# Two row-block pairs of the way up computed plainly, rows in memory laid out by operand, and the last group of the way down added on the chip

## The chip, the cores and the metric

The kernel runs on one core of a Trainium2 chip. The metric is the device time of one execution in microseconds. Before the change it was 2530.95 us as a median of three runs (2529.95 to 2533.86). The engines are named as in the profile: PE (TensorE, matmuls; PEld its weight loads), DVE (VectorE), ACT (ScalarE), POOL (GpSimd), SP (SyncE, which here issues DMAs).

## The reference

One step of a hybrid encoder layer for 1024 tokens of a prompt and 64 tokens of a running stream. The part that the change touches is the end of the layer, a gated feed-forward network with a short causal convolution:

```python
mix = jax.nn.sigmoid(gate_ssm) * (y_ssm @ p['w_branch_ssm']) + jax.nn.sigmoid(gate_att) * (o @ p['w_branch_attn'])
x = x + mix @ p['w_out']

h = _rmsnorm(x, p['norm_ffn_w']) @ p['w_up']
ha, hb = jnp.split(h, 2, axis=-1)
hc, ffn_new = _causal_dwconv(ffn_past, ha, p['ffn_conv_w'], p['ffn_conv_b'])
x = x + (jax.nn.silu(hc) * hb) @ p['w_down']
```

`D_MODEL` is 1024, `D_FF` is 2816, the convolution is three wide, and everything is float32.

## The kernel before

*Layout.* Tokens are columns, features are rows: the 1088 tokens lie side by side, and a tile holds 128 features. In the FFN the columns are cut into four quarters of 272 (`QW`); a half is two quarters. Quarter `2 * v + s` is quarter `s` of half `v`.

*Precision.* A float32 operand is split in two: `hi` is a cast by ACT to the matmul's rounded type, `lo` is the difference of the operand and `hi`, by DVE (`split`, L840 to L842). Each product of two tiles is three matmuls: hi·hi, hi·lo and lo·hi.

*Seven products for eight.* The FFN's two matrix products are done in blocks of two by two with seven products instead of eight (the Strassen-Winograd scheme). On the way up, an item is a pair: row block `f` of `w_up` and row block `f + 22`, the convolution's side and the gate's. The inner dimension has two halves of four tiles, the columns two halves. The right-hand operands (`PARTS`) are `b11`, `t2`, `b21`, `t3`, `t1`, `t4` and `b22`: quarters of x1, or sums and differences of them, made by `differences` (L895 to L905), split by `part`, and kept on the chip in the homes of a table (`home`; units are named n0 to n11 and m000 to m311). The left-hand operands are weight blocks or sums of them: `left_parts` loads two blocks of 512 KB, makes four sums on POOL (L918, L919, L929, L936) and splits seven operands of 128 x 512. A pair is 7 products x 2 quarters x 4 tiles x 3 = 168 matmuls of 272 columns.

*From x1 to the FFN.* `output(m, qs)` computes row block `m` of x1 for the quarters `qs`, adds the input, stores the rows to `yT` and has POOL add up squares. `norm(q)` multiplies the sum by a block of ones on PE (L875), and ACT and DVE make the reciprocal root (L211 to L215, with loads of activation tables, since Ln, Exp and Square alternate); then DVE scales eight tiles (L882). `first_half` does this for quarters 0 and 1 and splits `b11` and `b21` between the outputs of quarters 2 and 3. Quarters 2 and 3 are normed behind the last output. Pairs 0 and 1 are begun with their products p0 (`b11`) and p2 (`b21`), which need quarters 0 and 1 alone; their other five products need differences.

*A pair's end.* `pair(f)` takes each product's sum from PSUM with ACT or DVE (L1059 to L1078), `gate` applies the convolution and silu (an affine step on ACT, two on DVE, silu on ACT), `put` multiplies with the gate's side on POOL (L1051) and stores a half row block to `h_sc`.

*The way down.* The 22 hidden row blocks form three groups, `DOWN` = 8, 8 and 6. Each group is four items of two output row blocks, again seven products. `hidden_sums` loads the stored rows, makes the four right-hand sums on POOL (L989 to L992) and stores them to `t_sc`. `hidden_part(g, name)` loads the rows of an operand of the next group (`hr`), casts them on ACT (L1010) and subtracts on DVE, for the second quarter beyond the first two tiles on POOL (L1011). That is done while the last item of the previous stage runs, part by part, into the homes that its products leave. `pair_down` adds its results onto `yT` in memory by accumulating DMAs, issued by POOL (L1092), 48 in all, 16 per group.

*What sets the order.* The code names the engine of each instruction. A scheduler orders the instructions of each engine by the program's order, by priorities and by its own model of durations; each engine then runs its row in order. All loads and plain stores are issued by SP.

Of the kernel before, what the change touches and what calls it, by code (L numbers as in the profile page):

```python
# [9 lines left out]
F32 = mybir.dt.float32  # L10
# [7 lines left out]
P = 128  # L18
# [57 lines left out]
def hybrid_layer(ctx: ExitStack, tc: tile.TileContext, xT, prm, cst, rope, wvd, win, wbs, wba, wout, wup, wdn,  # L76
# [19 lines left out]
    h_sc = scratch("h_sc", [DFF, T])  # L96
    t_sc = scratch("t_sc", [4 * DFF // 2, T // 2])
# [792 lines left out]
    def differences(s, eng):  # L890

        b11, b21, b12, b22 = x1[s][:2], x1[s][2:], x1[2 + s][:2], x1[2 + s][2:]
        t2 = [couple(row("fs", "t2")) for _ in range(2)]
        for j in range(2):
            eng.tensor_tensor(out=b11[j], in0=b12[j], in1=b11[j], op=ALU.subtract)  # L895
        for j in range(2):
            V.tensor_tensor(out=t2[j], in0=b22[j], in1=b11[j], op=ALU.subtract)
        part("t2", s, t2)
        for j in range(2):
            G.tensor_tensor(out=b12[j], in0=b22[j], in1=b12[j], op=ALU.subtract)  # L900
        part("t1", s, b11)
# [4 lines left out]
        part("b22", s, b22)  # L906
# [67 lines left out]

# [3 lines left out]
    h3 = h_sc.rearrange("(f p) t -> p f t", p=P)  # L978
    t3 = t_sc.rearrange("(k f p) t -> p k f t", k=4, p=P)
    KIND = ("t1", "t2", "t3", "t4")  # L980

    def hidden_sums(i):

        b11, b12, b21, b22 = (row("fb", n)[:, :HALF] for n in ("g11", "g12", "g21", "g22"))
        e = row("fb", "ge")[:, :HALF]
        for u, (x, y) in enumerate(((b11, b12), (b21, b22))):
            for v, t in enumerate((x, y)):
                load(out=t, in_=h3[:, 2 * i + u, HALF * v : HALF * (v + 1)])
# [4 lines left out]
        for n, t in zip(KIND, (e, b11, b12, b21)):  # L993
            load(out=t3[:, KIND.index(n), i], in_=t)
# [138 lines left out]
    for at in early:  # L1133
        pairs[0].send(at)
        if at[1] == 1 and at[0] == 0:
            more_left(1)
# [133 lines left out]
```

## Time and profile before

| | |
|---|---|
| median of 3 runs | 2530.95 us (2529.95 to 2533.86) |
| the profiled execution | 2527.61 us |
| its span | 2525.8 us |
| mean granted TensorE clock | 0.986 |
| PE busy | 2440.0 us (97%), 16910 matmuls |
| DVE busy | 1612.5 us (64%) |
| ACT busy | 1184.8 us (47%) |
| POOL busy | 723.2 us (29%) |
| bytes moved | 399.15 MB |

Busy times are sums over one execution. The output stage ends at about 1760 us, the way up at about 2270 us, the way down with the span. A row of the timeline gives start, duration, engine, line, operation, output and inputs, the count of like instructions, and in brackets how long the engine stood before it and what ended that. A row by stretch gives the stretch, its length, and busy time and count of each engine, the granted clock, the share of the DMA engines and GB/s.

### The profile page before, as it was taken

What the parts mean: (1) busy time and instruction counts of PE and PEld (TensorE: products, weight loads), DVE (VectorE), ACT (ScalarE), POOL (GpSimd) and SP (SyncE); (2) the same over time, 40 slices, a digit from 0 to 9 for tenths busy, and PEclk for the clock granted to TensorE, in tenths of its full rate; (3) what the DMA queues carried; (4) which work ended last, traced back from release to release, by engine and by line L of the source; (5) the groups of instructions that cost most, each with busy time, mean ns of one, the idle gap of its engine ahead of it and who ended that gap; (6) DMA issues with size and microseconds to landing.
All of it is one profiled execution on the core that took longest, in us unless ns stands there. A gap on an engine that the chain in (4) does not pass through costs nothing. (4 is left out here: it accounts for less than half of the span.)

```text
span 2525.8 us, 44652 instructions
## 1 busy us (share of the span) xinstructions
PE 2440.0 (97%) x16910; PEld 2358.9 (93%) x16910; DVE 1612.5 (64%) x2724; ACT 1184.8 (47%) x2574; POOL 723.2 (29%) x745
## 2 busy tenths in 40 slices
PE   8999999999999999999999998998699999998998
PEld 8999999999999999998889898998699999998998
DVE  6326255854777667447667764645877777786764
ACT  6234243644666455357655754225443434343542
POOL 3000000100111001014433240024476676666543
PEclk9999999999999999999999999999799999999999
DMA  5217158545354354255697745663134333467875
GB/s 165 79 57 275 68 217 246 163 137 152 110 150 138 110 147 117 88 193 175 204 342 240 235 128 198 203 195 107 39 123 140 122 140 120 141 206 185 205 162 97
DMA packets 261911, 399.15 MB, mean 158 GB/s; under 512 B 32288, under 2 KB 190112, under 8 KB 261568
## 3 DMA queue, kind: packets, MB, share of 16 engines
q1 hardware_dynamic: 254784, 382.93, 47.3%
q0 software_dynamic: 6912, 13.37, 3.7%
q8 instruction: 133, 2.18, 0.4%
q14 instruction: 82, 0.67, 0.1%
HBM read 262.65 MB, written 133.56 MB: 157 GB/s over the span
## 5 line engine op out<-in xcount | busy, mean ns | idle before, releaser
L149 PE MATMUL mm<-xn_hi,w_hi 128*128 128x384 f32 (+1 forms) x1416 | 470.3, 332 | 0.9 <-DVE zr L431 0.9
L151 PE MATMUL mm<-xn_hi,w_lo 128*128 128x384 f32 (+1 forms) x1416 | 468.3, 331 | 0.5 <-DVE w_lo L143 0.5
L150 PE MATMUL mm<-xn_lo,w_hi 128*128 128x384 f32 (+1 forms) x1416 | 467.1, 330 | 0.0
L149 PEld LDWEIGHTS mm<-xn_hi,w_hi 128*128 128x128 f32 x1416 | 266.6, 188 | 5.3 <-issue 2.0
L151 PEld LDWEIGHTS mm<-xn_hi,w_lo 128*128 128x128 f32 x1416 | 266.7, 188 | 3.0 <-issue 0.8
L150 PEld LDWEIGHTS mm<-xn_lo,w_hi 128*128 128x128 f32 x1416 | 266.6, 188 | 1.8 <-issue 0.6
L143 DVE TENSOR_TENSOR w_lo<-w_f,w_hi 128x1024 fp32r<-128x1024 f32 (+1 forms) x120 | 152.7, 1273 | 127.6 <-ACT w_hi L142 127.1
L1023 PE MATMUL mx<-n,wh 128*128 128x272 f32 x1156 | 222.0, 290 | 6.2 <-ACT u L1101 2.3
L1023 PE MATMUL mx<-m,w_hi 128*128 128x272 f32 x1114 | 214.4, 290 | 7.0 <-DVE down L1109 5.3
L1023 PEld LDWEIGHTS mx<-n,wh 128*128 128x128 f32 x1156 | 182.8, 190 | 7.3 <-ACT u L1101 2.8
L142 ACT CAST w_hi<-w_f 128x1024 fp32r<-128x1024 f32 (+1 forms) x120 | 125.7, 1049 | 131.2 <-PE mm L150 74.5
L1023 PEld LDWEIGHTS mx<-m,w_hi 128*128 128x128 f32 x1114 | 177.3, 191 | 7.6 <-issue 5.1
L1023 PE MATMUL mx<-n,wl 128*128 128x272 f32 x578 | 167.2, 290 | 0.0
L1023 PE MATMUL mx<-m,w_lo 128*128 128x272 f32 x557 | 161.6, 290 | 0.0
L149 PE MATMUL mm<-b_hi,w_hi 128*128 128x384 f32 (+1 forms) x448 | 147.3, 330 | 6.5 <-DVE b_g L193 3.4
L151 PE MATMUL mm<-b_hi,w_lo 128*128 128x384 f32 (+1 forms) x448 | 146.5, 327 | 0.0
L150 PE MATMUL mm<-b_lo,w_hi 128*128 128x384 f32 (+1 forms) x448 | 146.3, 327 | 0.0
L448 POOL COPY pre<-pre 128x3 f32<-128x3 f32 x48 | 13.1, 273 | 456.3 <-ACT pre L449 332.5
L549 ACT ACTIVATE p_t<-sc,mx 128x1024 f32<-128x1024 f32 (+5 forms) x144 | 106.0, 738 | 76.6 <-DVE mx L540 36.5
L460 DVE SCALAR_TENSOR_TENSOR cc<-pre,par,cc 128x384 f32<-128x384 f32 (+1 forms) x216 | 126.5, 586 | 23.5 <-ACT cc L458 18.4
L841 ACT CAST w_hi<-ws 128x512 fp32r<-128x512 f32 (+1 forms) x68 | 41.4, 608 | 169.6 <-PE mx L1023 122.9
L842 DVE TENSOR_TENSOR wl<-w_f,wh 128x512 fp32r<-128x512 f32 (+1 forms) x102 | 94.7, 928 | 30.3 <-ACT wh L841 29.6
(346 smaller groups left out, 6730.2 us busy)
## 6 DMA issues: line engine op xcount, KB each, us to landing
w_f<-in_win_dram SPq DMA_DIRECT2D x76, 512.0 KB, 3.7
w_f<-in_wup_dram SPq DMA_DIRECT2D x44, 512.0 KB, 3.7
bc<-a_sc SPq DMA_DIRECT2D x32, 512.0 KB, 6.3
out_dram<-down POOLq DMA_DIRECT2D x48, 272.0 KB, 4.9
h_sc<-hb SPq DMA_DIRECT2D x44, 272.0 KB, 2.1
g<-h_sc SPq DMA_DIRECT2D x44, 272.0 KB, 3.7
hr<-t_sc SPq DMA_DIRECT2D x40, 272.0 KB, 4.7
x_sc<-cc SPq DMA_DIRECT2D x48, 192.0 KB, 2.1
```

The costliest lines, as they stand in the source:

```text
L142: S.copy(hi, w)
L143: V.tensor_tensor(out=lo, in0=w, in1=hi, op=ALU.subtract)
L149: PE.matmul(ps, a_hi, b_hi, start=i == 0, stop=False)
L150: PE.matmul(ps, a_hi, b_lo, start=False, stop=False)
L151: PE.matmul(ps, a_lo, b_hi, start=False, stop=i == n - 1)
L448: G.tensor_copy(pre[:, 0:3], tail)
L460: V.scalar_tensor_tensor(cc[:, :m], pre[:, i : i + m], cw(i), cc[:, :m], ALU.mult, ALU.add)
L549: act(p_t[:n, :nk], sc[c][:n, :nk], AF.Exp, bias=mx[:n, c : c + 1], accum_out=dst)
L841: S.copy(hi, src)
L842: V.tensor_tensor(out=lo, in0=src, in1=hi, op=ALU.subtract)
L1023: PE.matmul(ps, w[x][:, c], b[y][:, k], start=start and k == t == 0, stop=k == nk - 1 and t == 2, skip_group_check=not start)
```

## The change

Three things change.

1. *Pairs 0 and 1 are computed plainly*, with eight products: `pair_plain` does 192 matmuls per pair. `plain_left` loads their four weight blocks and splits them whole (128 x 1024), into the homes that `t2`, `t3` and `t4` of quarter 0 and `t2` of quarter 1 take later. The first half of each pair takes `b11` and `b21`. The second half takes `t1`, which is b12 − b11, added onto the first half's partial results, and `b22`. `first_differences` makes `t1` and splits `t1` and `b22`; `last_differences` makes and splits `t2`, `t3` and `t4`. The first halves of both pairs come first, then the last differences, then pair 2's weights, then the second halves.
2. *Rows in memory by operand.* `h_sc` and `t_sc` become one `q_sc` with eight kinds (`b11` to `b22`, `t1` to `t4`), each laid out by quarter, partition, row block and column. A load of an operand's two row blocks reads one run of 2176 B per partition, where it read two of 1088; a store of a half row and a load for `hidden_sums` now move two runs of 1088 B where they moved one of 2176. `hidden_part` subtracts on DVE throughout (21 of its 84 subtractions were on POOL).
3. *The last group of the way down is added on the chip.* Its items load their 16 half rows of `yT` early (`xr`). Product p2's two sums are taken by DVE with the addition, where ACT copied them; p3 is followed by an addition on POOL of 272 columns for each quarter, p4 and p5 by one of 544. SP stores the results; the 16 accumulating DMAs go.

On PE, the place behind the last output. Rows of `st` are the norms, n_18312, n_18585 before and n_18323, n_18596 after (with their neighbours) are `b11`, and `wh` and n_18090 to n_18097 weights of pair 0. Before:

```order
9521 L151 MATMUL mx<-m_16461,w_lo 128x272
9522 L875 MATMUL st_18733<-s_18095,con 128x272
9523 L875 MATMUL st_18790<-s_18126,con 128x272
9524 L1023 MATMUL mm<-n_18312,wh 128x272
9525 L1023 MATMUL mm<-n_18313,wh 128x272
9526 L1023 MATMUL mm<-n_18585,wh 128x272
```
After:

```order
9528 L150 MATMUL mx<-m_16460,w_lo 128x272
9529 L874 MATMUL st_18720<-s_18106,con 128x272
9530 L1095 MATMUL mm<-n_18324,n_18090 128x272
9531 L1095 MATMUL mm<-n_18323,n_18091 128x272
9532 L1095 MATMUL mm<-n_18323,n_18090 128x272
```
```order
9567 L1095 MATMUL mx<-n_18596,n_18097 128x272
9568 L1095 MATMUL mx<-n_18596,n_18096 128x272
9569 L874 MATMUL st_18751<-s_18137,con 128x272
9570 L1095 MATMUL mx<-n_18597,n_18096 128x272
9571 L1095 MATMUL mx<-n_18596,n_18097 128x272
```
The two norms stood together; now norm 3's matmul stands behind 39 plain ones.

On ACT, the same place; `sq` are squares of x1, `n` the norms' rows, `w_hi` a weight's cast. Before:

```order
1409 L841 CAST w_hi<-w_f 128x512
1410 L870 ACTIVATE sq<-x_18634 128x272
1411 L211 ACT_TABLE_LOAD
1412 L211 ACTIVATE n_18735<-st_18733,eps_t 128x272
1413 L870 ACTIVATE sq<-x_18634 128x272
1414 L212 ACT_TABLE_LOAD
1415 L212 ACTIVATE n_18736<-n_18735 128x272
1416 L213 ACTIVATE n_18735<-n_18736 128x272
1417 L211 ACT_TABLE_LOAD
1418 L211 ACTIVATE n_18792<-st_18790,eps_t 128x272
```
After:

```order
1413 L840 CAST w_hi<-w_f 128x512
1414 L869 ACTIVATE sq<-x_18645 128x272
1415 L210 ACT_TABLE_LOAD
1416 L210 ACTIVATE n_18722<-st_18720,eps_t 128x272
1417 L869 ACTIVATE sq<-x_18645 128x272
1418 L211 ACT_TABLE_LOAD
1419 L211 ACTIVATE n_18723<-n_18722 128x272
1420 L212 ACTIVATE n_18722<-n_18723 128x272
1421 L210 ACT_TABLE_LOAD
1422 L210 ACTIVATE n_18753<-st_18751,eps_t 128x272
1423 L840 CAST m_18745<-x_18409 128x544
1424 L211 ACT_TABLE_LOAD
```
The cast ahead of norm 2 is of pair 2's weights now (pair 0's before), and a cast of `b22` has come between norm 3's steps.

On POOL, after, where pair 1 ends and pair 2's weight sums begin; L1064 is `put`, L935, L936, L946 and L953 are the four weight sums:

```order
300 L1073 COPY con<-pre 128x2
301 L1048 MEMSET pre 128x2
302 L1064 TENSOR_TENSOR hb<-hb,cc 128x480
303 L1064 TENSOR_TENSOR hb<-hb,cc 128x64
304 L935 TENSOR_TENSOR ws_19086<-w_f 128x512
305 L936 TENSOR_TENSOR ws_19087<-ws_19086,w_f 128x512
306 L946 TENSOR_TENSOR w_f<-w_f 128x512
307 L953 TENSOR_TENSOR ws_19087<-w_f,ws_19087 128x512
308 L935 TENSOR_TENSOR ws_19388<-w_f 128x512
```
Before, the first weight sums behind the differences of quarters 2 and 3; L900 is a difference, L918, L919, L929 and L936 are the four sums, the first row of L936 the last sum of pair 0, the others of pair 1:

```order
294 L900 TENSOR_TENSOR x_18127<-x_18430,x_18127 128x544
295 L900 TENSOR_TENSOR x_18280<-x_18634,x_18280 128x544
296 L936 TENSOR_TENSOR ws_18702<-w_f,ws_18702 128x512
297 L1065 COPY pre<-pre 128x2
298 L918 TENSOR_TENSOR ws_18895<-w_f 128x512
299 L919 TENSOR_TENSOR ws_18896<-ws_18895,w_f 128x512
300 L929 TENSOR_TENSOR w_f<-w_f 128x512
```
Before, three of pair 0's sums stand ahead of the differences and pair 1's sums follow them; now no sum is made for pairs 0 and 1, and the first one stands behind pair 1's second `put`.

The diff, cut to its core:

```diff
@@ -887,23 +886,41 @@
             js = slice(2 * j, 2 * j + 2)
             split(hi[:, js], lo[:, js], src[j])
 
-    def differences(s, eng):
-
-        b11, b21, b12, b22 = x1[s][:2], x1[s][2:], x1[2 + s][:2], x1[2 + s][2:]
+    def quads(s):
+        return x1[s][:2], x1[s][2:], x1[2 + s][:2], x1[2 + s][2:]
+
+    def first_differences(s):
+
+        b11, b21, b12, b22 = quads(s)
+        for j in range(2):
+            V.tensor_tensor(out=b11[j], in0=b12[j], in1=b11[j], op=ALU.subtract)
+        part("t1", s, b11)
+        part("b22", s, b22)
+
+    def last_differences(s):
+
+        b11, b21, b12, b22 = quads(s)
         t2 = [couple(row("fs", "t2")) for _ in range(2)]
         for j in range(2):
-            eng.tensor_tensor(out=b11[j], in0=b12[j], in1=b11[j], op=ALU.subtract)
-        for j in range(2):
             V.tensor_tensor(out=t2[j], in0=b22[j], in1=b11[j], op=ALU.subtract)
-        part("t2", s, t2)
         for j in range(2):
             G.tensor_tensor(out=b12[j], in0=b22[j], in1=b12[j], op=ALU.subtract)
-        part("t1", s, b11)
+        part("t2", s, t2)
         part("t3", s, b12)
         for j in range(2):
             V.tensor_tensor(out=b21[j], in0=b21[j], in1=t2[j], op=ALU.subtract)
         part("t4", s, b21)
-        part("b22", s, b22)
+
+    def plain_left(f, homes):
+
+        w = []
+        for block, at in zip((wup[f], wup[f + FT]), homes):
+            src = wp.tile([P, WMAX], F32, name="w_f", tag="w_f", bufs=2)[:, :1024]
+            load(out=src, in_=block)
+            hi, lo = (unit(*u).rearrange("p a t -> p (a t)")[:, :1024] for u in home[at])
+            split(hi, lo, src)
+            w.append((hi, lo))
+        return w
 
@@ -960,38 +977,40 @@
     for m in range(KT):
         output(m, (0, 1))
     todo = first_half()
+    plain = [plain_left(0, (("t2", 0), ("t3", 0)))]
     for m, qs in *((m, (2, 3)) for m in range(6)), (6, (2,)), (7, (2,)), (6, (3,)), (7, (3,)):
         output(m, qs)
         next(todo, None)
     run(todo)
-    left = {0: list(left_of(0))}
-    coming = left_of(1)
-    run(norm(2))
-    differences(0, G)
-    run(norm(3))
-    differences(1, G)
+    plain.append(plain_left(1, (("t4", 0), ("t2", 1))))
+    left = {}
+    for s in range(2):
+        run(norm(2 + s))
+        first_differences(s)
...
-    h3 = h_sc.rearrange("(f p) t -> p f t", p=P)
-    t3 = t_sc.rearrange("(k f p) t -> p k f t", k=4, p=P)
-    KIND = ("t1", "t2", "t3", "t4")
+    KINDS = ("b11", "b12", "b21", "b22", "t1", "t2", "t3", "t4")
+    q5 = q_sc.rearrange("(n s p) (i t) -> n p s i t", n=8, s=2, t=QW)
+
+    def kind(name):
+        return q5[KINDS.index(name)]
@@ -1001,14 +1020,9 @@
             for j in range(0, nk, 2):
                 n = min(2, nk - j)
                 t = couple(row("fb", "hr"))[:, :n]
-                if name in KIND:
-                    src = t3[:, KIND.index(name), i0 + j : i0 + j + n, QW * s : QW * (s + 1)]
-                else:
-                    f, c = 2 * (i0 + j) + (name[1] == "2"), HALF * (name[2] == "2") + QW * s
-                    src = h3[:, f : f + 2 * n - 1 : 2, c : c + QW]
-                load(out=t, in_=src)
+                load(out=t, in_=kind(name)[:, s, i0 + j : i0 + j + n])
                 S.copy(hi[:, j : j + n], t)
-                (G if s and j else V).tensor_tensor(out=lo[:, j : j + n], in0=t, in1=hi[:, j : j + n], op=ALU.subtract)
+                V.tensor_tensor(out=lo[:, j : j + n], in0=t, in1=hi[:, j : j + n], op=ALU.subtract)
 
     def piles(i, nk):
         banks = {}
@@ -1049,7 +1062,63 @@
         def put(h, cc):
             for o, d, n in ((0, 0, 544),) if h == 0 else ((0, 0, 480), (480, 482, 64)):
                 G.tensor_tensor(out=hb[h][:, o : o + n], in0=hb[h][:, o : o + n], in1=cc[:, d : d + n], op=ALU.mult)
-            load(out=h_sc[P * f : P * (f + 1), 544 * h : 544 * (h + 1)], in_=hb[h][:, :544])
+            load(out=kind(("b11", "b12", "b21", "b22")[f % 2 * 2 + h])[:, :, f // 2], in_=couple(hb[h]))
+
...
+    def pair_plain(f, w):
+
+        pre, hb, u1, u2, put, end_first, end_second, to_second = pair_rows(f)
+        banks = {}
+
+        def pile(r, h, name, s, start, stop):
+            if start:
+                banks[r, s] = acc(QW)
+            ps = banks[r, s]
+            b = B[name, s]
+            for k in range(4):
+                c = slice(P * (4 * h + k), P * (4 * h + k + 1))
+                for t, (x, y) in enumerate(((0, 0), (0, 1), (1, 0))):
+                    PE.matmul(ps, w[r][x][:, c], b[y][:, k], start=start and k == t == 0, stop=stop and k == 3 and t == 2,
+                              skip_group_check=name == "b21")
+            return ps
+
+        yield
+        for s in range(2):
+            for r, u in enumerate((u1, u2)):
+                S.copy(u[:, s], pile(r, 0, "b11", s, True, True))
+            S.copy(pre[0][:, 2 + QW * s : 2 + QW * (s + 1)], pile(0, 1, "b21", s, False, True))
+            S.copy(hb[0][:, QW * s : QW * (s + 1)], pile(1, 1, "b21", s, False, True))
+        put(0, end_first())
+        yield
+        for s in range(2):
+            for r in range(2):
+                pile(r, 0, "t1", s, True, False)
+                ps = pile(r, 1, "b22", s, False, True)
+                if r == 0:
+                    to_second(ps, u1, s)
+                else:
+                    V.tensor_tensor(out=hb[1][:, QW * s : QW * (s + 1)], in0=ps, in1=u2[:, s], op=ALU.add)
+        end_second()
+        yield
+
+    def pair(f):
+
+        pre, hb, u1, u2, put, end_first, end_second, to_second = pair_rows(f)
...
     def pair_down(g, j):
...
-        c = {}
+        c, x = {}, {}
...
-
-        def put(m, h, t):
-            G.dma_start(out=yT[P * m : P * (m + 1), HALF * h : HALF * (h + 1)], in_=t, accum_op=ALU.add)
-
+        at_out = {2: (0, 0), 4: (1, 1), 5: (1, 0), 6: (0, 1)}
+        final = g + 1 == len(DOWN)
+
+        def place(p):
+            m, h = at_out[p]
+            return yT[P * (2 * j + m) : P * (2 * j + m + 1), HALF * h : HALF * (h + 1)]
+
+        if final:
+            for p in (2, 6, 4, 5):
+                x[p] = row("fb", "xr")[:, :HALF]
+                load(out=x[p], in_=place(p))
...
             elif p == 2:
-                S.copy(c[p][:, qs], pile("a", p, s, False))
+                ps = pile("a", p, s, False)
+                if final:
+                    V.tensor_tensor(out=c[p][:, qs], in0=ps, in1=x[p][:, qs], op=ALU.add)
+                else:
+                    S.copy(c[p][:, qs], ps)
...
                 V.tensor_tensor(out=u1[:, s], in0=pile("b", p, s, False), in1=u1[:, s], op=ALU.add)
+                if final:
+                    G.tensor_tensor(out=u2[:, s], in0=u2[:, s], in1=x[6][:, qs], op=ALU.add)
...
-            if s == 1 and p in (2, 4, 5, 6):
-                m, h = {2: (0, 0), 4: (1, 1), 5: (1, 0), 6: (0, 1)}[p]
-                put(2 * j + m, h, c[p])
+            if s == 1 and p in at_out:
+                if not final:
+                    G.dma_start(out=place(p), in_=c[p], accum_op=ALU.add)
+                else:
+                    if p in (4, 5):
+                        G.tensor_tensor(out=c[p], in0=c[p], in1=x[p], op=ALU.add)
+                    load(out=place(p), in_=c[p])
@@ -1127,27 +1209,21 @@
         if x is not None:
             left.setdefault(i, []).append(x)
 
-    pairs = [begun(0), begun(1)]
-    early = [(p, s) for p in (0, 2) for s in range(2)]
-    rest = [[(p, s) for s in range(2) for p in (1, 3, 4, 5, 6)], [(p, s) for p in (1, 3, 4, 5, 6) for s in range(2)]]
-    for at in early:
-        pairs[0].send(at)
-        if at[1] == 1 and at[0] == 0:
-            more_left(1)
-    for _ in range(2):
-        more_left(1)
-    for at in early:
-        pairs[1].send(at)
-    for i, at in enumerate(rest[0]):
-        pairs[0].send(at)
-        if i >= 6:
-            more_left(1)
-    left[1] += coming
-    for i, (g, f) in enumerate(work[1:], 1):
+    pairs = [pair_plain(f, plain[f]) for f in range(2)]
+    for u in pairs:
+        next(u)
+    for u in pairs:
+        next(u)
+    for s in range(2):
+        last_differences(s)
+    left[2] = list(left_of(2))
+    for u in pairs:
+        next(u)
+    for i, (g, f) in enumerate(work[2:], 2):
         coming = left_of(i + 1) if i + 1 < len(work) else iter(())
-        u = pairs[1] if i == 1 else begun(i)
+        u = begun(i)
         last = i + 1 < len(work) and work[i + 1][0] not in (g, None)
-        for p, s in rest[1] if i == 1 else [(p, s) for p in range(7) for s in range(2)]:
+        for p, s in [(p, s) for p in range(7) for s in range(2)]:
             u.send((p, s))
             if s == 1:
                 more_left(i + 1)
```

More of the change, by code (lines that the diff above doesn't have):

```diff
@@ L992, in hidden_sums @@
         G.tensor_tensor(out=b21, in0=b21, in1=b11, op=ALU.subtract)
-        for n, t in zip(KIND, (e, b11, b12, b21)):
-            load(out=t3[:, KIND.index(n), i], in_=t)
+        for n, t in zip(KINDS[4:], (e, b11, b12, b21)):
+            load(out=kind(n)[:, :, i], in_=t)
     def hidden_part(g, name):
@@ L1027, in piles, with pair_rows @@
         return pile
-    def pair(f):
+    def pair_rows(f):
         pre = [row("fp", "pre") for _ in range(2)]
@@ L1051, in put, with end_first, end_second @@
                 G.tensor_tensor(out=hb[h][:, o : o + n], in0=hb[h][:, o : o + n], in1=cc[:, d : d + n], op=ALU.mult)
-            load(out=h_sc[P * f : P * (f + 1), 544 * h : 544 * (h + 1)], in_=hb[h][:, :544])
+            load(out=kind(("b11", "b12", "b21", "b22")[f % 2 * 2 + h])[:, :, f // 2], in_=couple(hb[h]))
+        def end_first():
+            G.tensor_copy(pre[1][:, 0:2], pre[0][:, 544:546])
+            return gate(0)
+        def end_second():
+            G.tensor_copy(ffn_o[:, f, 0:2], pre[1][:, 480:482])
+            G.tensor_copy(ffn_o[:, f, 2:4], pre[1][:, 546:548])
+            put(1, gate(1))
@@ new lines, in to_second @@
+        def to_second(ps, u, s):
+            for o, d, n in ((0, 2, QW),) if s == 0 else ((0, 2 + QW, 208), (208, 484, 64)):
+                V.tensor_tensor(out=pre[1][:, d : d + n], in0=ps[:, o : o + n], in1=u[:, s, o : o + n], op=ALU.add)
+        return pre, hb, u1, u2, put, end_first, end_second, to_second
+    def pair_plain(f, w):
[30 more added lines that the diff above has]
+        yield
@@ L1076, in pair @@
                 ps = pile("c", p, s, False)
-                for o, d, n in ((0, 2, QW),) if s == 0 else ((0, 2 + QW, 208), (208, 484, 64)):
-                    V.tensor_tensor(out=pre[1][:, d : d + n], in0=ps[:, o : o + n], in1=u2[:, s, o : o + n], op=ALU.add)
+                to_second(ps, u2, s)
                 if s == 1:
-                    G.tensor_copy(ffn_o[:, f, 0:2], pre[1][:, 480:482])
-                    G.tensor_copy(ffn_o[:, f, 2:4], pre[1][:, 546:548])
-                    put(1, gate(1))
+                    end_second()
             at = yield
```

20 lines of the change are left out of this document (9 added, 11 removed).

## The prediction

> **What bounds the kernel now.** I read the page's first part, then busy time by stretch, then the timeline of each engine where a stretch falls short, and the transfers last.
>
> ```profile
> span 2525.8 us, 44652 instructions
> PE 2440.0 (97%) x16910; PEld 2358.9 (93%) x16910; DVE 1612.5 (64%) x2724; ACT 1184.8 (47%) x2574; POOL 723.2 (29%) x745
> ```
> ```profile
> 2300.00:2350.00 50.00, 50.00 (x401) 50.00 (x400) 27.86 (x43) 19.01 (x39) 26.82 (x23) 1.00 0.71 165
> 1759.40:1820.00 60.60, 33.61 (x198) 30.94 (x197) 49.26 (x70) 31.22 (x53) 25.21 (x20) 0.69 0.09 29
> 2245.00:2300.00 55.00, 42.94 (x310) 41.60 (x309) 51.24 (x58) 27.93 (x52) 39.40 (x30) 0.94 0.83 241
> 2350.00:2372.00 22.00, 17.80 (x122) 17.59 (x121) 22.00 (x29) 11.96 (x21) 12.14 (x10) 0.84 0.97 267
> 2450.00:2466.00 16.00, 14.14 (x108) 13.39 (x107) 12.94 (x25) 8.83 (x21) 10.40 (x11) 1.00 0.76 174
> ```
> PE bounds the program: 97% busy, and where it is full it does 401 recorded matmuls of 272 columns in 50 us, 0.1247 us each (columns: stretch, its length, PE, weight loads, DVE, ACT, POOL busy with counts, granted clock, DMA share). A shorter time therefore comes from fewer matmuls, or from the four stretches above in which PE falls short: the start of the FFN and the three changes of operands before the groups of the way down. Against 0.1247 us per matmul:
> - start: four of the 198 records belong to the two norms, 1.24 us at their unthrottled 0.62 us each (row below). 60.60 − 1.24 − 194 × 0.1247 = 35.2 us lost;
> - first change: 55.00 − 310 × 0.1247 = 16.3 us lost; second: 22.00 − 15.2 = 6.8; third: 16.00 − 13.5 = 2.5.
>
> Why PE stands at the start:
>
> ```profile
> 1759.40 0.62 PE L875 MATMUL st<-s,con 128*128 128x272 f32 x2
> 1763.69 1.25 PE L875 MATMUL st<-s,con 128*128 128x272 f32 x2 [3.67 <-DVE n L214]
> 1774.53 1.27 PE L1023 MATMUL mm<-n,wh 128*128 128x272 f32 x4 [9.60 <-ACT wh L841]
> 1780.91 0.60 PE L1023 MATMUL mm<-n,wl 128*128 128x272 f32 x1 [5.10 <-DVE wl L842]
> 1780.00:1800.00 20.00, 12.65 (x60) 11.70 (x61) 20.00 (x27) 10.05 (x19) 7.07 (x5) 0.57 0.16 53
> ```
> After the last output PE has nothing until norms, differences and pair 0's weight splits have passed through DVE, which is full for the whole of 1780 to 1800; and what PE does then runs at a clock of 0.57.
>
> **The change, part by part.** *Plain pairs, added work.* A plain pair has 8 products of 24 matmuls where a seven-product pair has 7, so 192 for 168. Two pairs: 48 × 0.1247 = +6.0 us, all on PE, hidden by nothing.
>
> *Plain pairs, the hole.* Their first halves are 192 matmuls, 23.9 us, and need only quarters 0 and 1 and four weight splits, which are issued during the last outputs. Norm 2, norm 3, the scales and t1 and b22 run beside them. The second halves, another 23.9 us, cover t2, t3, t4 and pair 2's weights. So the 35.2 us go, and what is late next has to be found. I walked PE's new row order against durations of these rows:
>
> ```profile
> 1758.02 1.28 ACT L211 ACT_TABLE_LOAD   x1
> 1760.06 0.49 ACT L211 ACTIVATE n<-st,eps_t 128x272 f32<-128x272 f32 x1 [0.76 <-PE st L875]
> 1763.10 0.44 DVE L214 SCALAR_TENSOR_TENSOR n<-st,n 128x272 f32<-128x272 f32 x1 [3.06 <-ACT n L213]
> 1773.87 0.61 ACT L841 CAST wh<-w_f 128x512 fp32r<-128x512 f32 x1
> 1848.95 2.38 POOL L1051 TENSOR_TENSOR hb<-hb,cc 128x480 f32<-128x480 f32 x2
> 1846.46 1.28 POOL L919 TENSOR_TENSOR ws<-ws,w_f 128x512 f32<-128x512 f32 x1
> 2272.09 0.85 ACT L1043 ACTIVATE cc<-pre,par 128x546 f32<-128x546 f32 x1 [1.79 <-POOL con L1080]
> 2277.64 0.77 DVE L1045 SCALAR_TENSOR_TENSOR cc<-pre,par,cc 128x546 f32<-128x546 f32 x1
> 2278.44 0.66 ACT L1046 ACTIVATE cc<-cc 128x546 f32<-128x546 f32 x1 [2.53 <-DVE cc L1045]
> 2516.84 0.44 DVE L1113 TENSOR_TENSOR down<-mx,u 128x272 f32<-128x272 f32 x1 [0.69 <-PE mx L1023]
> ```
> 1. A weight cast now stands ahead of norm 2's table load on ACT, and the last output's weights come after the added ones: about 0.7 us of PE.
> 2. Norm 3's matmul stands among the plain ones, 39 matmuls (4.9 us) behind norm 2's, in the same accumulator. It needs norm 2's read by DVE: two table loads and three activations of 0.4 to 0.5, with a square between and the cast ahead, 5 to 7 us. I take 1.7 us of PE, and 0.4 for the first eviction, which ACT does behind norm 3.
> 3. Pair 2's p4 weights. Their first sum stands on POOL behind pair 1's second put. From the end of the last plain matmul but 24 (3.0 us ahead of the end): three evictions 1.2, affine 0.85, two DVE steps 1.5, silu 0.66, put 2.4, sum 1.28, cast 0.61, split 0.7: 9.2 us, and PE has those 3.0 us and pair 2's first 24 matmuls, 3.0. That is 3.2, and 3.4 with a semaphore's few hundredths at each step.
> 4. After such a wait the clock falls:
>
> ```profile
> 2251.53 0.82 PE L1023 MATMUL mx<-m,wh 128*128 128x272 f32 x2 [2.37 <-DVE u L1061]
> 2251.53:2255.53 4.00, 4.00 (x20) 4.00 (x21) 4.00 (x4) 4.00 (x9) 3.51 (x2) 0.60 0.77 238
> 2262.39 0.52 PE L1023 MATMUL mx<-m,w_hi 128*128 128x272 f32 x2 [1.67 <-DVE hb L1070]
> 2262.39:2266.39 4.00, 4.00 (x32) 4.00 (x32) 4.00 (x8) 3.42 (x7) 2.19 (x1) 1.00 0.68 200
> ```
> The 2.37 us wait is followed by 4 us at 0.60 (20 matmuls where 32 fit, 1.5 us lost); the 1.67 us wait leaves the clock whole. So the 3.4 us wait costs 2.0 more, the 1.7 us one nothing. [...]
>
> New stalls: 0.7 + 1.7 + 0.4 + 3.4 + 2.0 = 8.2. Bounds: 0 if the chains run faster than I laid them, and 18 if each takes twice as long. Start: −35.2 + 6.0 + 8.2 = **−21.0** (−29.2 to −11).
>
> *Hidden-row splits and layout.* 21 POOL splits go to DVE, seven in each change.
>
> ```profile
> 2361.62 0.82 PE L1023 MATMUL mm<-m,w_hi 128*128 128x272 f32 x2 [4.20 <-DVE down L1109]
> L1011 POOL TENSOR_TENSOR m<-hr,m 128x544 fp32r<-128x544 f32 x5 | 8.7, 1738 | 0.9 <-ACT m L1010 0.9
> L1011 POOL TENSOR_TENSOR n<-hr,n 128x544 fp32r<-128x544 f32 x2 | 4.1, 2048 | 5.3 <-ACT n L1010 5.3
> 2287.45 1.65 POOL L1011 TENSOR_TENSOR m<-hr,m 128x544 fp32r<-128x544 f32 x1
> 2287.59 4.56 DVE L842 TENSOR_TENSOR wl<-w_f,wh 128x512 fp32r<-128x512 f32 x1
> 2292.43 0.68 DVE L842 TENSOR_TENSOR wl<-w_f,wh 128x512 fp32r<-128x512 f32 x1
> 2361.49 0.71 DVE L1011 TENSOR_TENSOR m<-hr,m 128x544 fp32r<-128x544 f32 x1
> h_sc<-hb SPq DMA_DIRECT2D x44, 272.0 KB, 2.1
> ```
> In the first change DVE is full (51.24 of 55 us) and evictions queue behind its splits. A split is 0.68 to 0.71 us alone and 4.56 beside three POOL operations. DVE gains 7 × 0.65 = 4.5 us of work, and 12.8 us of POOL work that slowed it goes. [...] Not all of the 12.8 lay beside a DVE split (POOL waited 6.2 us around them), so I take about 60% of it, 7.5 − 4.5 = 3 us. Ends: +4.5 (no contention goes) and −8.3. In the second change PE waits on DVE, which waits for operand rows; the new loads read one run of 2176 B per partition, not two of 1088. I take −3 of its 6.8, −1 of the third's 2.5. Ends +2 and −5, +0.5 and −2. The stores and the loads for the hidden sums are cut in two instead; they lie under a PE that is full, so nothing. Changes: **−7** (+7 to −15).
>
> *Last group.*
>
> ```profile
> out_dram<-down POOLq DMA_DIRECT2D x48, 272.0 KB, 4.9
> 2475.00:2500.00 25.00, 25.00 (x201) 25.00 (x200) 12.40 (x27) 6.71 (x17) 13.63 (x14) 1.00 0.52 93
> 2517.64 0.29 PE L1023 MATMUL mx<-m,w_lo 128*128 128x272 f32 x1
> 2518.70 0.86 POOL L1092 DMA_DIRECT2D out_dram<-down  x1 [1.40 <-DVE down L1113]
> ```
> Sixteen POOL issues of 0.86 us go; 16 POOL adds, 8 DVE evictions in ACT's stead and 16 loads come. PE is full here and DVE half idle (12.40 of 25), so I cost them at nothing; if that cover were gone, eight evictions of 0.44 would be 3.5. At the end 7.1 us lie between the last issue's start and the end of the span. A plain store from SP takes about 2.1 to land where the accumulating one takes 4.9; issue and interval differ little, so 2.8, less 0.3 for the semaphore to SP: **−2.5** (−1 to −4).
>
> Sum: −21.0 − 7 − 2.5 = −30.5 on the profiled execution's 2527.61 us (span 2525.8 and 1.8 around it): 2497.1. That execution is 3.3 below the median of 2530.95, so about 2501 as a median.
>
> **The rivals.**
> [...]
> *The wait moves.* The four engines' chain from norm 2 to t4 stays the bound of pair 2 and the stalls are doubled: −11 − 4 − 2.5 = −17.5, about 2513. For it: DVE is full there today. Against: 47.8 us of matmuls now lie over the same work.
> *DVE chokes at the changes.* 21 more splits on an engine that is full, and no contention goes: −21 + 7 − 2.5 = −16.5, about 2514. For it: DVE 51.24 of 55. Against: the 4.56 beside the 0.68.
> *Slower: pair 2 never gets its lead back.* If its late sums make pair 3's late, and so on, each of the 20 pairs to come waits. At 1.7 us a pair, which leaves the clock whole, that is 34 us on the −30.5: 2535. It decides from 1.5 us a pair. Against: the same POOL work per pair runs today in full stretches,
>
> ```profile
> 1820.00:1840.00 20.00, 20.00 (x162) 20.00 (x161) 14.81 (x23) 6.79 (x11) 11.31 (x11) 1.00 0.24 81
> ```
> right after a start that was later still.
>
> **How the numbers follow.** My forecast 0.45; hole wholly closed 0.17; wait moves 0.15; DVE chokes 0.11; several losses that just cancel the gain 0.05; slower 0.07. About 0.2%, 5 us, can be told from no change here. All but the last two are faster by more: 0.88, same 0.05, slower 0.07. The likeliest gives 2501, with its own range 2492 to 2509; the cases at 2487, 2513 and 2514 widen that to 2486 to 2518, which leaves the last two and the tails outside.
>
> **What would show it.** Right: no wait of over 4 us on PE between the last output and 1830; norm 3's matmul waits 1 to 2 us on DVE; pair 2 waits about 3 us on the split of its summed weights, behind POOL's put; the stretch of the first change has over 330 matmuls in 55 us; the span ends some 5 us after the last DVE step's start. Wrong: a standing PE at the beginning of the second halves (t1 or b22 late), DVE steps of over 4 us in the changes with POOL idle, or evictions in the last group behind POOL's adds.

## The result and the profile after

The changed kernel takes 2494.39 us as a median of four runs (2491.97 to 2499.35), beside 2530.45 us before. The ratio is 0.9857, 95% interval 0.9835 to 0.9878: 36 us faster. The forecast was 2501 with a range from 2486 to 2518.

The profiled execution is the slowest of the four, 2499.35 us. The first step of the output stage (DVE's, on the first row block) comes at 1673.7 us where it came at 1667.7 before, although the instructions up to there stand in the same order. Over the kernels below it lies between 1667.3 and 1674.0, with variants of the changed kernel at both ends. So these 6.0 us are not put down to the change, and what follows compares stretches behind that point.

The first part of the changed kernel's page:

```profile
span 2497.2 us, 44757 instructions
PE 2441.4 (98%) x16958; PEld 2361.0 (95%) x16958; DVE 1592.7 (64%) x2735; ACT 1181.6 (47%) x2564; POOL 691.4 (28%) x712
```
Its busy time by stretch (the first row is 6.0 us later than its counterpart before, the others follow the pairs and items):

```profile
1765.40:1826.00 60.60, 55.67 (x433) 54.88 (x432) 45.95 (x75) 35.87 (x64) 30.84 (x27) 0.99 0.10 33
2231.30:2286.30 55.00, 49.57 (x368) 48.69 (x367) 47.59 (x68) 29.81 (x55) 32.22 (x25) 0.94 0.83 262
2319.80:2383.90 64.10, 63.62 (x507) 63.27 (x506) 48.10 (x79) 31.98 (x61) 28.55 (x25) 1.00 0.82 215
```
The start's 60.6 us now hold 433 matmuls where 198 stood, at a clock of 0.99. At 0.1247 us each, 60.60 − 1.24 − 429 × 0.1247 = 5.9 us are lost, for 35.2. The 55 us at the first change of operands hold 368 for 310. Some of PE's waits that are left, those that the text names:

```profile
1773.48 0.70 PE L874 MATMUL st<-s,con 128*128 128x272 f32 x2 [1.19 <-DVE n L213]
1779.16 1.01 PE L1095 MATMUL mm<-n,n 128*128 128x272 f32 x6 [0.73 <-ACT u L1102]
1823.63 0.77 PE L1037 MATMUL mm<-m,w_hi 128*128 128x272 f32 x4 [3.01 <-ACT w_hi L840]
2246.04 0.52 PE L1037 MATMUL mx<-m,w_hi 128*128 128x272 f32 x2 [1.97 <-DVE hb L1138]
2273.00 0.82 PE L1037 MATMUL mx<-m,w_hi 128*128 128x272 f32 x2 [2.06 <-DVE down L1187]
2338.09 0.52 PE L1037 MATMUL mm<-m,w_hi 128*128 128x272 f32 x2 [0.48 <-DVE down L1187]
2430.61 0.52 PE L1037 MATMUL mx<-n,wh 128*128 128x272 f32 x2 [1.45 <-ACT u L1173]
2441.63 0.52 PE L1037 MATMUL mx<-m,w_hi 128*128 128x272 f32 x2 [1.73 <-DVE down L1187]
2459.12 0.52 PE L1037 MATMUL mm<-m,w_hi 128*128 128x272 f32 x2 [1.42 <-DVE down L1187]
```
PE waits 1.19 us at norm 3, 0.73 for the first eviction (a product's sum taken out of PSUM), and 3.01 for the weights of pair 2's product p4: the three places of the forecast, in its order. 4.93 and 4.20 us in the changes of operands have become 2.06 and 0.48. The last three, 4.6 us together, stand in the last group; the first of them has a counterpart of 0.92 before, the other two are new. The end, from the timeline of all engines:

```profile
2493.01 0.29 PE L1037 MATMUL mx<-m,w_lo 128*128 128x272 f32 x1
2493.04 1.17 SPq L1198 DMA_DIRECT2D out_dram<-down  x2
2493.41 0.44 DVE L1191 TENSOR_TENSOR down<-mx,u 128x272 f32<-128x272 f32 x1 [0.70 <-PE mx L1037]
```
From the last matmul's end to the end of the span lie 3.9 us, for 7.9.

The table by stretch serves all that follows. Its marks are the first step of the output stage on DVE (out), the first eviction by ACT of a pair or item (pairs counted from 0 to 21, items of the way down from 0 to 11), the last matmul (PE) and the end of the span, read off each kernel's timeline, one execution each, in us.

| stretch | before | changed | plain | layout | DVE splits | last group | plain + DVE splits | changed again |
|---|---|---|---|---|---|---|---|---|
| out to pair 5 | 236.3 | 216.2 | 217.0 | 236.5 | 234.6 | 237.2 | 216.4 | 214.9 |
| pair 5 to pair 20 | 315.1 | 315.5 | 314.8 | 315.3 | 315.4 | 315.1 | 315.0 | 315.0 |
| pair 20 to item 2 (first change) | 100.7 | 93.4 | 100.3 | 99.9 | 92.9 | 100.0 | 91.6 | 92.2 |
| item 3 to item 6 (second) | 70.3 | 64.1 | 69.3 | 69.2 | 66.5 | 69.7 | 66.5 | 64.3 |
| item 7 to item 8 (third) | 25.3 | 25.2 | 25.0 | 25.9 | 24.8 | 26.1 | 24.3 | 23.7 |
| item 8 to the last matmul | 60.4 | 63.1 | 60.3 | 60.2 | 59.6 | 60.4 | 59.5 | 59.8 |
| last matmul to the end | 7.9 | 3.9 | 7.4 | 7.4 | 7.4 | 4.2 | 7.4 | 3.9 |

Items 2 to 3 and 6 to 7 take 21.1 us in all of them. Before to changed: −20.1, +0.4, −7.3, −6.2, −0.1, +2.7 and −4.0, −34.6 in sum.

### The profile page after: what moved, and what is told of

The parts are those of the page before. It is cut to its first block, busy times and chain, and to the rows that moved or that the text cites. A ratio compares the mean times of both kernels' runs of the same rounds, so it can differ in the third digit from the quotient of the medians.

```text
span 2497.2 us, 44757 instructions
## 1 busy us (share of the span) xinstructions
PE 2441.4 (98%) x16958; PEld 2361.0 (95%) x16958; DVE 1592.7 (64%) x2735; ACT 1181.6 (47%) x2564; POOL 691.4 (28%) x712
## 5 line engine op out<-in xcount | busy, mean ns | idle before, releaser
L1037 PE MATMUL mx<-n,wh 128*128 128x272 f32 x1092 | 209.5, 289 | 2.1 <-ACT u L1173 1.5
L1037 PE MATMUL mx<-m,w_hi 128*128 128x272 f32 x1050 | 202.8, 290 | 6.4 <-DVE down L1187 3.8
L1037 PEld LDWEIGHTS mx<-n,wh 128*128 128x128 f32 x1092 | 171.9, 189 | 2.7 <-ACT u L1173 1.7
L1037 PEld LDWEIGHTS mx<-m,w_hi 128*128 128x128 f32 x1050 | 166.9, 190 | 7.6 <-DVE down L1187 4.2
L1037 PE MATMUL mx<-n,wl 128*128 128x272 f32 x546 | 157.6, 289 | 0.0
L1037 PE MATMUL mx<-m,w_lo 128*128 128x272 f32 x525 | 152.4, 290 | 0.0
L686 POOL TENSOR_SCALAR_AFFINE_SELECT bc<-bc 128x1024 f32<-128x1024 f32 (+1 forms) x36 | 39.7, 1104 | 261.4 <-ACT e L673 261.4
```

Of the source, the lines that this page charges most:

```text
L686: G.affine_select(bc[:L, :, :L], bc[:L, :, :L], [[0, 8], [1, L]], ALU.is_ge, -1e30, base=0, channel_multiplier=-1)
L1037: PE.matmul(ps, w[x][:, c], b[y][:, k], start=start and k == t == 0, stop=k == nk - 1 and t == 2, skip_group_check=not start)
```

## The experiments

Each ratio is to runs of the kernel before taken beside it, with its 95% interval. A split is the subtraction that makes `lo`.

**One part at a time, added to the kernel before.** The plain pairs alone are the changed kernel with `q_sc`, `hidden_part` and `pair_down` put back. The layout alone and the last group alone are their parts of the diff. The DVE splits alone are one line:

```diff
-                (G if s and j else V).tensor_tensor(out=lo[:, j : j + n], in0=t, in1=hi[:, j : j + n], op=ALU.subtract)
+                V.tensor_tensor(out=lo[:, j : j + n], in0=t, in1=hi[:, j : j + n], op=ALU.subtract)
```
The plain pairs:

> Kernel before with pairs 0 and 1 computed plainly and nothing else changed. Theory (the parts add up): the start gives about -20 us, since the first matmuls of pair 4 came 14.2 us earlier in the changed kernel's trace, which was 6.0 us late when the output stage began; the three changes of operands keep their losses of about 16, 7 and 2.5 us and the tail its 7.9 us after the last matmul: about 2510. Rival (the plain pairs also ease the changes, by leaving the later pairs more lead): about 2500.

2507.60 us, ratio 0.9914 (0.9899 to 0.9929): 21.8 us faster than before. The table puts 19.3 us of it at the start and 1.4 in the first two changes. The parts add up here; the rival falls.

> Kernel before with rows laid out by operand and nothing else; 21 splits stay on POOL. Rival L (the gain of 13.6 us in the first two changes comes from faster loads): the hr loads land in about 4.3 us instead of 4.7, the waits in the first two changes shrink to about 5.5 and 0.5 us, about -13 us: 2517. Theory S (it comes from the splits that left POOL): waits as before, within 3 us of 2530.

> Kernel before with all splits of the hidden rows on DVE and nothing else; the old layout. Theory S (POOL's splits lock DVE and delay evictions): waits of PE in the first two changes go from 12.1 and 4.2 us to about 5.5 and 0.5, about -13 us: 2517. Rival L: within 3 us of 2530. Third case (DVE chokes): over 2533.

The layout: 2528.22 us, ratio 0.9999 (0.9987 to 1.0012), nothing. The DVE splits: 2516.15 us, ratio 0.9951 (0.9932 to 0.9969), 12.4 us faster. So most of the gain in the changes comes from the splits that left POOL; the longer runs in memory brought nothing by themselves (0.9999). How it comes is seen in busy time by stretch, the first and the second change of the kernel before, and then the same with DVE splits alone:

```profile
2219.10:2319.80 100.70, 88.64 (x674) 87.30 (x673) 80.37 (x101) 43.40 (x82) 66.84 (x55) 0.97 0.76 221
2340.90:2411.20 70.30, 66.10 (x506) 65.89 (x506) 50.65 (x72) 32.54 (x62) 38.44 (x32) 0.95 0.79 196
```
```profile
2219.00:2312.00 93.00, 87.68 (x674) 86.83 (x673) 72.40 (x108) 43.90 (x83) 56.98 (x48) 0.96 0.79 240
2333.00:2399.60 66.60, 64.06 (x506) 63.40 (x506) 48.14 (x79) 32.28 (x62) 28.56 (x25) 1.00 0.81 207
```
DVE (the third pair of numbers) does seven instructions more in each stretch and is busy 8.0 and 2.5 us less. POOL loses 9.9 us in each.

In the second change the layout does count once the splits are on DVE: 66.5 us in the two kernels with DVE splits and the old layout, 64.1 and 64.3 with the new one, and between 64.0 and 64.7 in the five variants of the changed kernel below. One of these, with the last group undone (64.7), differs from the plain pairs with DVE splits by the layout alone. That is about 2 us, which no run of the layout alone can show. It is seen in PE's waits for ACT's evictions in the second change, here with the plain pairs, DVE splits and the old layout:

```profile
2340.02 0.52 PE L1041 MATMUL mx<-n,wh 128*128 128x272 f32 x2 [0.86 <-ACT u L1170]
2344.46 0.51 PE L1041 MATMUL mx<-n,wh 128*128 128x272 f32 x2 [1.16 <-ACT u L1170]
```
Shortly ahead of the second, a cast on ACT waited 1.92 us for rows from memory; in the changed kernel it waits 0.23 there. With the new layout these waits of PE are 0.22 us or less in all seven executions.

> Kernel before with the last group added on the chip and nothing else. Theory: the end gains 3 to 4 us (4.2 us from the last matmul to the end of the span instead of 7.9), and the last group loses about 2.7 us again, because weight loads land late beside the added loads of the output rows: PE waits of 1.4 to 1.7 us inside the last group that the kernel before does not have; the net is -1 us, within 0.2% of before. Rival (the waits in the last group belong to the other parts): -4 us, 2526.

2524.63 us, ratio 0.9983 (0.9972 to 0.9994), 4.3 us faster; 3.7 us of it behind the last matmul. The stretch from item 8 to the last matmul does not grow (60.4). The rival was right here: taken alone, the last group brings its full gain.

**Two parts together.**

> Kernel before with the plain pairs and with all splits of hidden rows on DVE; rows in memory and the last group as before. If the parts add, -21.8 from the one and -12.4 from the other: 0.9865 of before, about 2495, with the first changes of operands at about 93 and 66 us (pair 20 to third item, fourth to seventh item) and 7.4 us behind the last matmul. If the layout has a share that shows only beside the other two (the stretch from the fourth to the seventh item took 64.1 in the changed kernel and 66.5 with the splits alone), it is 2 to 3 us slower than the changed kernel there.

2496.03 us, ratio 0.9877 (0.9861 to 0.9894), 31 us faster, where the two parts alone give 34; the intervals allow both. The stretches are those of the parts, and 66.5 us in the second change is the case of the layout's share.

**Double the POOL splits.** In the kernel before, 42 of the 84 splits on POOL:

```diff
-                (G if s and j else V).tensor_tensor(out=lo[:, j : j + n], in0=t, in1=hi[:, j : j + n], op=ALU.subtract)
+                (G if s else V).tensor_tensor(out=lo[:, j : j + n], in0=t, in1=hi[:, j : j + n], op=ALU.subtract)
```


> Kernel before with 42 instead of 21 splits of hidden rows on POOL. Theory S (a POOL operation that reads its operands beside a DVE split holds that split up for about its own length): DVE does seven splits less in the first change and is nevertheless busy longer, over 90 us instead of 86.3 in the stretch from pair 20 to the third item, which takes 105 to 109 us instead of 100.7; in all 10 to 14 us slower, 2541. Rival (POOL's splits are late, not in DVE's way, or DVE is short of time): DVE is busy some 5 us less and the stretch is not longer, 2520 to 2532.

2537.32 us, ratio 1.0038 (1.0025 to 1.0051), 9.6 us slower. Busy time of the two changes in this kernel:

```profile
2219.10:2317.30 98.20, 88.05 (x674) 87.00 (x673) 81.70 (x94) 43.51 (x83) 77.92 (x62) 0.97 0.76 224
2338.30:2419.40 81.10, 68.99 (x506) 68.54 (x506) 60.25 (x65) 32.60 (x62) 50.20 (x39) 0.89 0.68 171
```
In the second change DVE does seven instructions less and is busy 60.25 us for 50.65, and the stretch takes 81.1 us for 70.3. The whole chain shows there, from POOL's splits over DVE's to PE:

```profile
2354.74 2.91 POOL L1011 TENSOR_TENSOR n<-hr,n 128x544 fp32r<-128x544 f32 x2
2357.36 2.85 POOL L1011 TENSOR_TENSOR m<-hr,m 128x544 fp32r<-128x544 f32 x2
2353.65 7.15 DVE L1011 TENSOR_TENSOR n<-hr,n 128x544 fp32r<-128x544 f32 x2
2361.81 0.82 PE L1023 MATMUL mm<-m,w_hi 128*128 128x272 f32 x2 [6.98 <-DVE down L1109]
```
Two splits on DVE, 1.35 us where POOL is idle (with all splits on DVE), take 7.15 beside POOL's, and PE waits 6.98 us for the eviction behind them. In the first change, DVE is busy 81.70 for 80.37 with seven less, but the stretch is 2.5 us shorter, not longer as expected (the expectation's 86.3 and its "over 90" are sums of single durations, which overlap a little; by that sum it stays under 90 too). That POOL's splits hold up DVE is shown by DVE's busy time in all three doses: with none, 21 and 42 of them on POOL, and seven instructions less on DVE at each step, 72.40, 80.37 and 81.70 us in the first change and 48.14, 50.65 and 60.25 in the second. That this alone sets the length of the first stretch is not: with seven splits more on POOL there it should have grown. What shortened it is open.

**The wait before pair 2's p4.** In the first kernel the homes of `t2` and `t4` of quarter 1 are exchanged; in the second only pair 1's second `put` is on DVE.

```diff
-                                 (0, "b22"), (1, "t2"), (1, "t3"), (1, "t1"), (1, "t4"), (1, "b22"))]
+                                 (0, "b22"), (1, "t4"), (1, "t3"), (1, "t1"), (1, "t2"), (1, "b22"))]
-    plain.append(plain_left(1, (("t4", 0), ("t2", 1))))
+    plain.append(plain_left(1, (("t4", 0), ("t4", 1))))
```
```diff
-                G.tensor_tensor(out=hb[h][:, o : o + n], in0=hb[h][:, o : o + n], in1=cc[:, d : d + n], op=ALU.mult)
+                (V if f == 1 and h else G).tensor_tensor(out=hb[h][:, o : o + n], in0=hb[h][:, o : o + n], in1=cc[:, d : d + n], op=ALU.mult)
```


> Changed kernel with the homes of t2 and t4 of quarter 1 exchanged, so that pair 1's fourth weight block lies in t4's home. Theory B (pair 2's first weight sum waits for the buffers of t2 of quarter 1, whose split waits for the last plain matmul to leave its home): the sum goes ahead of pair 1's second put, the wait of 3.0 us before pair 2's p4 and the 3.4 us at half clock behind it go, -4 to -5 us against the changed kernel, about 2490. Theory P (the put itself holds it, as the prediction had it): the sum is behind the put's inputs anyway, and the wait stays between 2 and 3.5 us, 2494.

> Changed kernel with pair 1's second put on DVE instead of POOL. Theory P (the put holds POOL's first sum): POOL is free 2.0 us earlier, the wait goes from 3.0 to about 1 us and the clock stays whole, -3.5 us. Theory B (the buffers of t2 hold it): the sum starts where it did, within 0.3 us of the split of t2, and the wait stays at 2.5 to 3.5 us.

POOL's timeline of the changed kernel, and then POOL's and PE's with the put on DVE:

```profile
1819.69 2.02 POOL L1064 TENSOR_TENSOR hb<-hb,cc 128x480 f32<-128x480 f32 x2 [0.53 <-ACT cc L1059]
1821.67 1.26 POOL L935 TENSOR_TENSOR ws<-w_f 128x512 f32<-128x512 f32 x1
```
```profile
1815.26 1.71 POOL L935 TENSOR_TENSOR ws<-w_f 128x512 f32<-128x512 f32 x1 [0.82 <-DVE m L841]
```
```profile
1817.68 0.78 PE L1037 MATMUL mm<-m,w_hi 128*128 128x272 f32 x4 [1.73 <-ACT w_hi L840]
```
In the changed kernel the sum follows the put without a gap. Without the put, PE waits 1.73 us for 3.01, not about 1 as expected, and POOL's sum now waits for DVE's split of `t2`, whose buffers it takes. So both theories hold a part: the put comes last, and behind it stand the buffers, which let the sum start 1.7 us sooner (1.0 us behind the start of silu on ACT, for 2.7). The two are not independent: DVE's two splits of `t2` take 2.37 us beside POOL's put, where the two of quarter 0 take 1.35 with no put beside them. The run takes 2489.42 us, 0.9841 (0.9826 to 0.9855).

With the homes exchanged the sum does go ahead of the put, and the wait of 3.0 us goes, but PE waits later instead:

```profile
1829.57 0.52 PE L1037 MATMUL mx<-n,wh 128*128 128x272 f32 x2 [1.22 <-DVE u L1130]
1841.38 0.52 PE L1037 MATMUL mx<-m,w_hi 128*128 128x272 f32 x2 [2.51 <-DVE hb L1138]
```
From out to pair 5 it takes 216.9 us, as much as the changed kernel. The wait has moved; 2492.12 us, 0.9850 (0.9834 to 0.9866), and the 4 to 5 us expected do not show.

**The last group.** First the loads of output rows are spread over an item, then the whole part is undone.

```diff
-        if final:
-            for p in (2, 6, 4, 5):
-                x[p] = row("fb", "xr")[:, :HALF]
-                load(out=x[p], in_=place(p))
         at = yield
         for _ in range(14):
             p, s = at
             qs = slice(QW * s, QW * (s + 1))
+            if final and s == 0 and p < 4:
+                o = (2, 6, 4, 5)[p]
+                x[o] = row("fb", "xr")[:, :HALF]
+                load(out=x[o], in_=place(o))
```


> Changed kernel with the last group's loads of output rows spread over the item's first four products instead of at its begin. Theory D (they delay the weight loads of the last group, in SP's queue and on the DMA engines): the waits of 1.45, 1.73 and 1.42 us in the last group shrink below 0.8 us each, -2 to -3 us. Rival (the result stores in SP's queue hold the weight loads): waits as in the changed kernel, no gain.

> Changed kernel with the last group added by accumulating DMAs as before. If the last group's waits are its own doing, the stretch from the last item but four to the last matmul takes about 85.5 us as in the kernel before instead of 88.3, and from the last matmul to the end 7.4 instead of 3.9: +0.7 us, a change without a net effect in this combination. If the waits are those of the other parts, it is 3.5 us slower than the changed kernel, 2498.

Spread: 2489.03 us, 0.9840 (0.9825 to 0.9855); from item 7 to the last matmul 84.8 us for the changed kernel's 88.3. Undone: 2490.73 us, 0.9853 (0.9838 to 0.9867); 83.6 us there and 7.4 behind the last matmul. Both read as if the waits in the last group came from the added loads. The next run takes most of that reading away.

**The changed kernel again, and the two gains together.**

> The changed kernel again, beside the next one. 2491 to 2496; the wait of 3.0 us before pair 2's p4 and some 4.6 us of waits in the last group come back. Whether 3.4 us at half clock follow the wait of 3.0 is open: they did in one profile of the changed kernel and did not in the variant with the last group undone, after a wait of 2.98.

> Changed kernel with pair 1's second put on DVE and the last group's loads of output rows spread over the item. The two gains lie in different stretches, so they should add: -2.2 us at the start, -3.5 in the last group, and the changed kernel's half clock behind the first wait gone: 2487, 5 to 7 us under the changed kernel.

The changed kernel again: 2490.69 us, 0.9847 (0.9833 to 0.9862). Both gains: 2491.48 us, 0.9846 (0.9830 to 0.9861), where 2487 was expected; no sum of gains shows. The second execution of the unaltered kernel has no waits in its last group at all, by stretch from 2400 us to its last matmul:

```profile
2400.00:2486.00 86.00, 85.83 (x681) 85.33 (x679) 61.03 (x116) 30.86 (x69) 41.14 (x37) 1.00 0.65 199
```
From item 7 to the last matmul it takes 83.5 us, as with the part undone (83.6). So the 4.6 us of waits in the first profile do not come with every execution of the same kernel. Their places say more. The wait of 1.45 us where the group begins stands in thirteen of the fourteen traces, from 0.43 to 1.95 us, the kernel before included; it is not the added loads'. The wait of 1.42 us stands in this execution alone. The wait of 1.73 us, inside item 8 before a matmul that DVE's eviction of p4 releases, stands in six of the seven executions with the last group added on the chip, from 0.46 (spread loads) to 1.73 us; without that part it stands only in the kernel with double POOL splits (1.16). So it does come with that part, in most executions; what sets its size is open. None of the variants can be told from the changed kernel by its total.

## Why the prediction was right

The direction, the range and the order of the three gains held; the total was undersized by 6 us, and most of the fault is in one term, the changes of operands.

- *The start, −21.0.* Measured −20.1 and −21.4 in two executions of the changed kernel, −19.3 for the plain pairs alone. The parts of the 8.2 us: norm 3 1.19 (1.7 forecast), the first eviction 0.73 (0.4), pair 2's p4 3.01 (3.4), and the low clock behind it 1.7 in the first execution and nothing in the second (2.0). The last output's weights cost 0.30 us where 0.7 was put. These parts alone would give −22.3 and −24.0, so the −20.1 and −21.4 hold some 2 us of loss that the sum had no term for; 1.1 and 1.2 of them are PE's waits for DVE's sums between pair 2 and pair 5. That −21.0 came so close is in part luck. The chain through pair 1's put was the last to arrive, as it was laid out; what it did not have is a second holder, the buffers of `t2`, 1.7 us ahead of it.
- *The changes of operands, −7: the step that was mis-sized.* Measured −7.3, −6.2 and −0.1 in the first execution, −8.5, −6.0 and −1.6 in the second. In the first change, where −3 was forecast, the step was "about 60%" of POOL's 12.8 us: the share of POOL's time that held up DVE. With the DVE splits alone, DVE's busy time fell by 8.0 us while it took seven more splits of 0.65, which is 12.5 us back against the 12.8 us of POOL splits that left: in this stretch nearly all of it (in the second change 7.1 us of DVE's time, and POOL's busy time fell by 9.9). All of the 12.8 us less the 4.5 of added splits would have been 8.3 net, the far end that the prediction gave this term; the run showed 8.0 of DVE time and 7.8 us of the stretch. The 6.2 us for which POOL waited around those splits were no reason to lower the share. In the second change the prediction had the wrong cause: it put its −3 down to rows that load faster. The layout alone left the wait of 4.2 us where it was (4.21), the splits alone took 3.8 us off the stretch, and the layout counted only beside them, for about 2.
- *The layout's stores and the loads for the hidden sums, nothing.* The layout alone changed nothing (0.9999).
- *The tail, −2.5.* Measured −4.0 and −3.7 against the 7.9 us of the kernel before, −3.5 against the 7.4 of the other kernels with the old end. The term compared median landings (4.9 and 2.1 us); the last accumulating transfer took 7.1 us from its issue to the end of the span, and the last plain store ended 3.4 us behind the DVE step that released it. No run shows the 0.3 put for the semaphore to SP: SP issues that store at 2493.88, 0.03 us behind the end of the DVE step.
- *The last group's adds, nothing.* Not quite settled. From item 7 to the last matmul six executions with them take 83.5 to 88.3 us, two without them 83.6 and 83.8, and the wait inside item 8 comes with them. The totals cannot be told apart (2490.69 and 2490.73).
- *The rivals.* "DVE chokes" falls: seven more splits, 8 us less busy. "Pair 2 never gets its lead back" falls: from pair 5 to pair 20 all kernels take 315 us. The case at 2487, the hole wholly closed, was half right: 12.5 of the 12.8 us came back in the first change, but steps 1 to 3 did cost (0.30, 1.19 and 0.73, and 3.01 us). "The wait moves" falls: the three stalls had about the forecast sizes, not twice as much.

## What to carry to other kernels

Where a matmul engine stands because its operands need sums that are not yet made, plainly computed products with operands that are ready can cost less than the wait: 6.0 us of added matmuls bought 26 to 27 us of standing (20.1 to 21.4 net). An elementwise step given to POOL to relieve a full DVE can cost DVE more than it takes off (here DVE took seven splits back in the first change and was busy 8.0 us less); compare DVE's busy time with and without it, not the instruction counts. And one profile of a kernel is not enough to call a wait of 1 to 2 us its own (the wait of 1.42 us stood in one execution of the changed kernel and not in the other): run the unaltered kernel again beside the variants.

## What was not expected of the hardware

The prediction took a wait of 2.37 us followed by a low clock (0.60) as a sign that waits from there on throttle. The runs show that in this range the length alone doesn't decide. Four us behind the same wait before pair 2's p4 (3.01, 2.98 and 2.97 us) in the changed kernel, in the one with the last group undone, and in the changed kernel again:

```profile
1823.63:1827.63 4.00, 4.00 (x22) 4.00 (x23) 3.86 (x4) 1.76 (x3) 3.37 (x3) 0.67 0.00 0
```
```profile
1818.11:1822.11 4.00, 4.00 (x32) 4.00 (x33) 3.86 (x4) 1.77 (x3) 3.37 (x3) 1.00 0.00 0
```
```profile
1824.15:1828.15 4.00, 4.00 (x32) 4.00 (x32) 3.86 (x4) 1.77 (x3) 3.38 (x3) 1.00 0.00 0
```
And behind a wait of 2.06 us before the same matmul of the first change, in the changed kernel and in the one with the last group undone:

```profile
2273.00:2277.00 4.00, 4.00 (x17) 4.00 (x18) 2.63 (x6) 0.00 (x0) 2.51 (x3) 0.50 0.93 241
```
```profile
2265.08:2269.08 4.00, 4.00 (x32) 4.00 (x33) 3.06 (x8) 0.74 (x2) 2.52 (x3) 1.00 0.90 247
```
In the changed kernel's first execution the clock has a mean of 0.72 over the 6 us behind the first of these waits and of 0.51 over the 6 us behind the other, which is 1.7 and 2.9 us lost; in its second execution nothing is lost behind the first. In the profiles of the kernel before and of the changed kernel alone, the other waits behind the last output part at 2.0 us: in the 4 us behind waits of 1.67, 1.73 and 1.97 us the clock is 1.00, behind 2.01, 2.19 and 2.37 us it is 0.50, 0.66 and 0.60, and behind six of 3.24 to 9.60 us it is 0.50 to 0.62 (some of these began at a low clock). But behind the waits of 2.06, 2.98 and 2.97 us above it is 1.00 too, and the same wait of about 3.0 us goes both ways in two executions of one kernel. What decides beside the length is open.
